# A hybrid decoder layer on one core: another order of the convolution, the compression's inputs and the compression in the input projection

## The chip, the core and the metric

The kernel runs on one core of a Trainium2 chip. The metric is device time in microseconds (us) from launch to the end of the program; several runs are made, and their median is told. The core's engines work side by side: TensorE (matrix products; PE in the profile, its weight loads PEld), VectorE (DVE), ScalarE (ACT), GpSimd (POOL) and SyncE (SP), which here only issues transfers. Each has its own queue of instructions and waits at semaphores for the others.

## The reference, cut to what matters

The layer takes a residual stream `x` of 512 positions and 2048 channels. It normalises it, multiplies it with one large input matrix `w_in`, and splits the columns of the product:

```python
proj = x @ w_in
q, k_c, v_c, k_s, v_s, k_w, v_w, g, u = jnp.split(proj, cuts, axis=-1)
gates = jax.nn.sigmoid(g)
kc = compress(kv_heads(k_c), cmp_pe_k, cmp_w1_k, cmp_w2_k)
vc = compress(kv_heads(v_c), cmp_pe_v, cmp_w1_v, cmp_w2_v)
o_nsa = nsa_attention(q, kc, vc, k_s, v_s, k_w, v_w, gates, rel_table)
o_conv = conformer_conv(u, conv_dw_w, conv_dw_b, conv_ln_g, conv_ln_b)
mix = jnp.concatenate([o_nsa, o_conv], axis=-1) @ w_out
```

`compress` takes windows of 32 positions of `k_c` (or `v_c`), multiplies them with a 2048x256 matrix, applies Gelu and multiplies with a 256x64 matrix. `conformer_conv` takes the 2048 columns `u`, multiplies one half with the Sigmoid of the other, applies a causal depthwise convolution of 31 taps to each of the 1024 channels, normalises over the channels and applies SiLU. Behind the mixer follow a cross-attention into 256 memory tokens and a mixture of 32 experts. The change touches only the order of work inside the input projection.

## The kernel before, in words

**One group of the projection.** `proj` (L102) computes up to 512 columns for all 512 positions. It loops over the 2048 input channels in 8 pieces of 256 (for a width of 512). For each piece `wtile` (L86) loads the weights into a ring buffer `wr` (three buffers, queue of SyncE) and splits them into a high and a low half, `wh` by ScalarE and `wl` by VectorE (L78, two buffers each). Each product is made of three (L82 to L84: high by high, high by low, low by high). They accumulate in four PSUM banks `pd`, one for each 128 columns, and a piece takes 24 products of 128x512. So a group takes 192. At the end `evac` empties the four banks. `hooks` names a function that is called before a given piece's weights; with it other work is laid between the pieces.

**The lead stage.** `mixer` (L330) loads `x`, normalises it, and `norm_T` (L166) turns it into 16 transposed chunks `xT`: four transposes (L172) into one of two PSUM banks of the tag "s", then ScalarE (L175) and VectorE (L176) read the bank, and VectorE subtracts (L177). The first group of the projection runs while these chunks come up. Then the pool `lnin` of the raw input closes, and other pools open: `cnv` for the convolution, `work`, and `cmp` for the compression.

**The compression's inputs.** `cmp_inputs` (L474) first clears `kcc` and `vcc` on GpSimd (L476, L477), loads and transposes the position vectors, and then runs the group for `k_c` and `v_c` (L503). It is the first group before the change. Its `evac` writes `kt` with 16 copies on ScalarE and 16 subtractions on VectorE (L501, L502).

**The convolution.** `conv_taps` (L409) loads the depthwise weights into a `wr` buffer (L414) and bias and norm vectors on GpSimd's queue (L417), transposes them on TensorE (L420, L423) into "s" banks, and copies them out to `wc` and `cvT` (L421, L424). Then it runs four groups of 512 columns: 256 of the first half and the matching 256 of the second. The eviction of a group makes two blocks of 128 channels. For each it takes the Sigmoid on ScalarE (L435), one of three `u` buffers, cleared at its head by GpSimd (L437), the product on VectorE (L438), which empties the two banks, and then 31 taps on VectorE (L441 and 30 times L443).

**The work between.** The generator `todo` chains `gate` (L508, two parts of 16 products), `compress` (L550, eight steps for keys and values, four each, of 24 products with 160 columns) and `mem_stats` (L275, four steps of statistics of the memory). The hooks of the convolution's groups take one step each: pieces 1 to 7 of group 0 and all pieces of the later groups. What is left is done behind group 3.

**Behind it** come `bias_setup`, `values` (L536, one group), `queries` for four heads (L595, groups of 384 columns, three banks, 144 products), and `conv_norm` (L447). The latter sums the channels with products against ones (L453, one pair of products for each block, `cmu`), subtracts the mean on VectorE (L459), squares, sums again (L462, `cvr`), and scales. From the second queries on, hooks bring in the transposed memory (`mem_T`, L289).

**What sets the order.** The program text gives each instruction a priority, and the builder fixes each engine's order from it, from readiness and from free buffers. `high_priority` with a positive offset moves instructions ahead, as for the weight splits and the first part of `conv_norm`; the taps have an offset of -100000, so they take what VectorE has left over:

```python
with tc.high_priority(offset=-100000):
    nc.vector.tensor_scalar(a, u[:, 0:S], wc[:, j, 0:1], vT[:, j:j + 1], op0=ALU.mult, op1=ALU.add)
    for k in range(1, CK):
        nc.vector.scalar_tensor_tensor(a, u[:, k:k + S], wc[:, j, k:k + 1], a, op0=ALU.mult, op1=ALU.add)
```

Of the kernel before, what the change touches and what calls it, by code (L numbers as in the profile page):

```python
# [22 lines left out]
S = 512  # L23
# [5 lines left out]
CW, CK = 1024, 31  # L29
# [23 lines left out]
class Kernel:  # L53
# [276 lines left out]
    def mixer(self):  # L330
        tc, nc, I = self.tc, self.nc, self.i
        w = I["w_in"][0]
        xh = lambda k, c: self.xT[k][:, 0, :] if c is None else self.xT[k][:, 0, c * P:(c + 1) * P]
        xl = lambda k, c: self.xT[k][:, 1, :] if c is None else self.xT[k][:, 1, c * P:(c + 1) * P]
        with ExitStack() as ctx:
            with ExitStack() as p1:
                self.psum(p1, d=4, s=2, t=1, o=1)
                xpb = p1.enter_context(self.pool("xpb", 6, True))
                xpa = p1.enter_context(self.pool("xpa", 10, True))
                with self.pool("lnin") as ln:  # L340
                    xs = [ln.tile([P, D], F32, name=f"xin{i}") for i in range(4)]
                    for i in range(4):
                        nc.sync.dma_start(xs[i], I["x"][0, i * P:(i + 1) * P, :])
                    gb = self.columns(ln, [I["ln_in_g"], I["ln_in_b"]], "xgb")
                    self.xT = [self.pg(xpa if k < 10 else xpb, f"xT{k}") for k in range(KC)]
                    for i in range(4):
                        self.normalise(xs[i], self.ln_stats(xs[i], self.inrs[:, i]))
                    self.norm_T(lambda i, k: xs[i][:, k * P:(k + 1) * P], 4, gb[:, 0], gb[:, 1], lambda k: (self.xT[k][:, 0, :], self.xT[k][:, 1, :]), ln, 6)
                cctx = p1.enter_context(ExitStack())
                cnv = cctx.enter_context(self.pool("cnv", 2, True))  # L350
                self.mctx = ExitStack()
                self.work = self.mctx.enter_context(self.pool("work"))
                self.kcc = self.work.tile([P, 2, NKV, 32], F32R, name="kcc")
                self.vcc = self.work.tile([32, NKV, P], F32R, name="vcc")
                self.gates = self.work.tile([P, 4, 48], F32, name="gates")
                with self.pool("cmp") as cp:
                    kt = self.cmp_inputs(cp, xh, xl, w)

                    todo = chain(self.gate(cp, xh, xl, w), self.compress(cp, kt), self.mem_stats())
                    kt = None  # L360
                    acc = self.conv_taps(cnv, xh, xl, w, lambda: next(todo, None))
                    for _ in todo:
                        pass
                self.bias_setup()
                self.mgb = self.columns(self.work, [I["mem_ln_g"][0], I["mem_ln_b"][0]], "mgb")
                vp = self.mctx.enter_context(self.pool("vp"))
                self.values(vp, xh, xl, w)
                self.kq = [self.queries(0, w, xh, xl)]
                self.conv_norm(acc, cnv)
                acc = None  # L370
                cctx.close()
                self.mpool = self.mctx.enter_context(self.pool("memT"))
                self.memT = []
                mt = p1.enter_context(self.pool("mtmp"))
                mem = lambda k: (lambda: self.mem_T(k, self.mpool, mt))
                for kv, hooks in ((1, HOOKS[0]), (2, HOOKS[1]), (3, {})):
                    self.kq.append(self.queries(kv, w, xh, xl, {n: mem(k) for n, k in hooks.items()}))
                self.xT = None

            with ExitStack() as p2:  # L380
                self.psum(p2, d=3, t=2, s=2, o=1)
                mp2 = self.mctx.enter_context(self.pool("memT2", 1, True))
                self.bmp = p2.enter_context(self.pool("bm", 3, True))
                self.kvp = p2.enter_context(self.pool("kvp", 2, True))
                self.mem_T(12, mp2, self.kvp, "t")
                self.att = p2.enter_context(self.pool("att", 2, True))
                self.mixT, self.heads = [None] * KC, []
                for kv in range(NKV):
                    pairs = self.attention(kv)
                    self.kq[kv] = None  # L390
                    if kv % 2 == 0:
                        m = self.bigt(0, f"mix{kv}")
                    for j in range(2):
                        k = 2 * kv + j
                        t = self.mixT[k] = m[:, k % 4]
                        self.split(t[:, 0, :], t[:, 1, :], pairs[j])
                self.wprio = 0
                for g in range(12):

                    h = PACE[g]  # L400
                    with tc.issue_after(self.heads[h].ins) if h >= 0 else ExitStack():
                        self.kv_group(g, "dve")
                self.wprio = 100000
        if "mix" in self.dbg:
            for k in range(KC):
                self.dump("mix", self.mixT[k].bitcast(F32), lambda a: a[k])


    def conv_taps(self, cnv, xh, xl, w, step):  # L409
        tc, nc, I = self.tc, self.nc, self.i  # L410
        wc = cnv.tile([P, 8, CK], F32, name="wc", bufs=1)
        vT = self.cvT = cnv.tile([P, 24], F32, name="cvT", bufs=1)
        nat = self.ring.tile([P, 1024], F32, tag="wr", bufs=self.RB, name="wr")[:CK]
        nc.gpsimd.dma_start(nat, I["conv_dw_w"][0].rearrange("k o c -> k (o c)"))  # L414
        vn = cnv.tile([24, P], F32, tag="sg", bufs=2, name="cvn")
        for j, nm in enumerate(("conv_dw_b", "conv_ln_g", "conv_ln_b")):
            nc.gpsimd.dma_start(vn[8 * j:8 * j + 8, :], I[nm][0].rearrange("(c p) -> c p", p=P))  # L417
        pt = self.ps()
        for c in range(8):
            nc.tensor.transpose(pt[:, c * 32:c * 32 + CK], nat[:, c * P:(c + 1) * P], self.ident[:CK, :CK])  # L420
        nc.vector.tensor_copy(wc, pt[:, :256].rearrange("p (c k) -> p c k", k=32)[:, :, :CK])  # L421
        pt = self.ps()
        nc.tensor.transpose(pt[:, :24], vn, self.ident[:24, :24])  # L423
        nc.vector.tensor_copy(vT, pt[:, :24])  # L424
        acc = [cnv.tile([P, 2, S], F32, name=f"acc{j}", bufs=1) for j in range(4)]
        for g in range(4):
            banks = {}

            def evac(c, bank):
                banks[c] = bank  # L430
                if c < 2:
                    return
                j = 2 * g + c - 2
                sg = cnv.tile([P, S], F32, tag="sg", bufs=2, name="sg")
                nc.scalar.activation(sg, bank, AF.Sigmoid)  # L435
                u = cnv.tile([P, CK - 1 + S], F32, tag="u", bufs=3, name="u")
                nc.gpsimd.memset(u[:, :CK - 1], 0.0)  # L437
                nc.vector.tensor_tensor(u[:, CK - 1:], banks[c - 2], sg, op=ALU.mult)  # L438
                a = acc[j // 2][:, j % 2, :]
                with tc.high_priority(offset=-100000):  # L440
                    nc.vector.tensor_scalar(a, u[:, 0:S], wc[:, j, 0:1], vT[:, j:j + 1], op0=ALU.mult, op1=ALU.add)  # L441
                    for k in range(1, CK):
                        nc.vector.scalar_tensor_tensor(a, u[:, k:k + S], wc[:, j, k:k + 1], a, op0=ALU.mult, op1=ALU.add)  # L443
            self.proj([(w, 2608 + 256 * g, 256), (w, 2608 + CW + 256 * g, 256)], 512, xh, xl, evac, False, 4, S, lo="dve", hooks={n: step for n in range(1 - min(g, 1), 8)})
        return acc

    def conv_norm(self, acc, work):  # L447
# [940 lines left out]
```

## Time and profile before

| what | value |
|---|---|
| median of 3 runs | 2642.68 us (2636.26 to 2644.41) |
| the profiled execution | 2640.3 us |
| its span, first to last instruction | 2638.5 us |
| TensorE busy | 2400.6 us |
| VectorE busy | 1136.0 us |
| ScalarE busy | 732.1 us |
| GpSimd busy | 192.9 us |
| mean granted TensorE clock | 0.964 |

Times in the rows count from the start of the span. "Busy" of an engine is the time in which it executed at least one instruction. A row of the timeline gives start, duration, engine, line, operation, tiles (written <- read), shapes and count; in square brackets stands how long the engine idled before it and what released it. A table by windows gives the same by stretches of time, with the granted clock of TensorE (1.00 is 2.4 GHz, 0.50 is 1.2 GHz) and the share of the 16 DMA engines.

### The profile page before, as it was taken

Reading aid. Unit: us, or ns where it says so; the run is one execution under the profiler, and the core shown is the slowest. Engines: PE = TensorE matmul, PEld = TensorE weight load, DVE = VectorE, ACT = ScalarE, POOL = GpSimd, SP = SyncE. Lnnn points to the kernel's source line nnn. Section 1 sums busy time; section 2 is a strip of 40 time slices with the busy share of each in tenths; the row PEclk is TensorE's granted clock in tenths of the full one; section 3 lists DMA queues with packets and bytes.
Section 4 is the critical chain, followed back from the end, with each engine's and each line's share of the span. In section 5 each row is a group of like instructions: output and inputs, shape, how many; then the busy total and the mean of one; then the engine's idle time right before and its main releaser. Section 6 shows DMA issues by size and latency. Waiting matters only on the chain. (4 is left out here: it accounts for less than half of the span.)

```text
span 2638.5 us, 31466 instructions
## 1 busy us (share of the span) xinstructions
PE 2400.6 (91%) x11314; PEld 1561.4 (59%) x11315; DVE 1136.0 (43%) x2406; ACT 732.1 (28%) x1294; POOL 192.9 (7%) x247
## 2 busy tenths in 40 slices
PE   6998898989999999999999968999998899999982
PEld 5786676779878778788888843333332334333320
DVE  5479985487877654543462442111110101101004
ACT  4332125376766522332321310101000001011003
POOL 1100000000000000000000120101000100111001
PEclk9999999999999999999999969999999999999996
DMA  3345233433234532333442397999999999999994
GB/s 138 102 141 160 72 79 108 122 108 121 92 117 129 198 128 96 135 106 101 180 155 97 120 372 314 417 416 411 407 409 406 412 398 415 340 403 414 415 411 165
DMA packets 194679, 615.22 MB, mean 233 GB/s; under 512 B 43147, under 2 KB 92483, under 8 KB 140978
## 3 DMA queue, kind: packets, MB, share of 16 engines
q1 hardware_dynamic: 176900, 563.90, 56.2%
q0 software_dynamic: 17296, 46.66, 5.8%
q8 instruction: 117, 1.92, 0.3%
q10 hardware_dynamic: 288, 2.10, 0.2%
q14 instruction: 78, 0.64, 0.1%
HBM read 591.56 MB, written 47.23 MB: 242 GB/s over the span
## 5 line engine op out<-in xcount | busy, mean ns | idle before, releaser
L1271 PE MATMUL gu<-mr,xeT 128*64 128x512 f32 x2048 | 542.2, 615 | 51.5 <-DMA mr<-moe_w_up 20.5
L78 DVE TENSOR_TENSOR wl<-wr,wh 128x1024 fp32r<-128x1024 f32 (+1 forms) x248 | 294.2, 1188 | 388.3 <-ACT wh L78 384.0
L78 ACT ACTIVATE wh<-wr 128x1024 fp32r<-128x1024 f32 (+1 forms) x250 | 256.0, 1026 | 633.3 <-PE pd L83 291.8
L1271 PEld LDWEIGHTS gu<-mr,xeT 128*64 128x64 f32 x2048 | 170.9, 140 | 358.3 <-issue 285.8
L1299 PE MATMUL dn<-mr,hT 128*64 128x512 f32 x1152 | 293.8, 601 | 14.5 <-PEq L1179 13.4
L1280 DVE TENSOR_TENSOR h<-gu,sg 64x256 f32<-64x256 f32 x72 | 30.7, 427 | 455.4 <-ACT sg L1279 454.8
L82 PE MATMUL pd<-xT,wh 128*128 128x512 f32 x512 | 201.9, 401 | 5.5 <-DVE v L546 2.2
L83 PE MATMUL pd<-xT,wh 128*128 128x512 f32 x512 | 204.0, 399 | 0.0
L1299 PEld LDWEIGHTS dn<-mr,hT 128*64 128x64 f32 x1152 | 91.0, 137 | 169.8 <-issue 151.5
L84 PE MATMUL pd<-xT,wl 128*128 128x512 f32 x512 | 183.6, 397 | 4.4 <-DVE wl L78 4.4
L1279 ACT ACTIVATE sg<-gu 64x256 f32<-64x256 f32 x72 | 27.0, 375 | 546.3 <-PE gu L1271 529.9
L443 DVE SCALAR_TENSOR_TENSOR acc<-u,wc,acc 128x512 f32<-128x512 f32 x240 | 164.2, 744 | 0.1
L1305 DVE TENSOR_SCALAR y<-dn,wlm 128x512 f32<-128x512 f32 x36 | 27.0, 751 | 228.4 <-PE dn L1299 212.2
L82 PEld LDWEIGHTS pd<-xT,wh 128*128 128x128 f32 x512 | 97.9, 191 | 31.6 <-issue 7.4
L84 PEld LDWEIGHTS pd<-xT,wl 128*128 128x128 f32 x512 | 97.1, 190 | 26.4 <-DVE wl L78 5.1
L1201 POOL DMA_INDIRECT acc_d<-y,ixm x36 | 56.9, 1580 | 731.3 <-DVE xeT L72 314.9
L83 PEld LDWEIGHTS pd<-xT,wh 128*128 128x128 f32 x512 | 97.4, 190 | 21.7 <-issue 2.4
L83 PE MATMUL pd<-x1T,wh 128*128 128x512 f32 x256 | 102.1, 400 | 0.0
L83 PE MATMUL pd<-wl,oT 128*128 128x512 f32 x256 | 100.0, 391 | 1.1 <-DVE wl L78 1.1
L84 PE MATMUL pd<-x1T,wl 128*128 128x512 f32 x256 | 100.9, 399 | 0.0
L82 PE MATMUL pd<-x1T,wh 128*128 128x512 f32 x256 | 99.2, 401 | 0.8 <-ACT x1T L175 0.8
L84 PE MATMUL pd<-wh,oT 128*128 128x512 f32 x256 | 99.8, 390 | 0.0
(414 smaller groups left out, 3954.4 us busy)
## 6 DMA issues: line engine op xcount, KB each, us to landing
mr<-moe_w_down SPq DMA_DIRECT2D x128, 1024.0 KB
mr<-moe_w_gate SPq DMA_DIRECT2D x127, 1024.0 KB
mr<-moe_w_up SPq DMA_DIRECT2D x127, 1024.0 KB
wr<-xa_wkv SPq DMA_DIRECT2D x64, 512.0 KB
wr<-w_in SPq DMA_DIRECT2D x112, 256.0 KB
wr<-w_out SPq DMA_DIRECT2D x32, 512.0 KB
wr<-xa_wq SPq DMA_DIRECT2D x32, 512.0 KB
wr<-xa_wo SPq DMA_DIRECT2D x32, 512.0 KB
```

The source lines that it names most:

```text
L78: return self.nc.scalar.activation(h, src, AF.Copy), eng.tensor_tensor(l, src, h.bitcast(F32), op=ALU.subtract)
L82: mm(out, lhsT=ah, rhs=bh, start=start, stop=False)
L83: mm(out, lhsT=ah, rhs=bl, start=False, stop=False)
L84: mm(out, lhsT=al, rhs=bh, start=False, stop=stop)
L443: nc.vector.scalar_tensor_tensor(a, u[:, k:k + S], wc[:, j, k:k + 1], a, op0=ALU.mult, op1=ALU.add)
L1201: self.nc.gpsimd.indirect_dma_start(out=self.acc_d.rearrange("s (h d) -> (s h) d", h=2), out_offset=bass.IndirectOffsetOnAxis(ap=ix, axis= ...
L1271: self.nc.tensor.matmul(bank[64 * a:64 * a + 64], lhsT=xT[:, 4 * q + c, :], rhs=w[a][:, c * 512:(c + 1) * 512], start=(q == c == 0), stop= ...
L1279: nc.scalar.activation(sg[64:128, sl], bank[0:64, sl], AF.Silu)
L1280: nc.vector.tensor_tensor(h[64 * b:64 * b + 64], bank[64:128, sl], sg[64:128, sl], op=ALU.mult)
L1299: self.nc.tensor.matmul(out[j][64 * a:64 * a + 64], lhsT=hT[:, r, :], rhs=w[:, 1024 * a + 512 * j:1024 * a + 512 * j + 512], start=(r == 0 ...
L1305: self.nc.vector.tensor_scalar(y[:, 512:], out[1], wl, None, op0=ALU.mult)
```

## The change

The convolution's weights are loaded and its group 0 runs first, in the lead stage, without hooks. Then `between` runs the compression's inputs and builds the chain of gate, compression and memory statistics. Groups 1 to 3 follow, each with a hook before each of its eight pieces. Nothing is added to or taken from the computation.

```diff
@@ mixer
                 with self.pool("cmp") as cp:
-                    kt = self.cmp_inputs(cp, xh, xl, w)
-
-                    todo = chain(self.gate(cp, xh, xl, w), self.compress(cp, kt), self.mem_stats())
-                    kt = None
-                    acc = self.conv_taps(cnv, xh, xl, w, lambda: next(todo, None))
-                    for _ in todo:
+
+                    todo = []
+
+                    def between():
+                        kt = self.cmp_inputs(cp, xh, xl, w)
+                        todo.append(chain(self.gate(cp, xh, xl, w), self.compress(cp, kt), self.mem_stats()))
+                    acc = self.conv_taps(cnv, xh, xl, w, lambda: next(todo[0], None), between)
+                    for _ in todo.pop():
                         pass
@@ conv_taps
-    def conv_taps(self, cnv, xh, xl, w, step):
+    def conv_taps(self, cnv, xh, xl, w, step, between):
...
-            self.proj([(w, 2608 + 256 * g, 256), (w, 2608 + CW + 256 * g, 256)], 512, xh, xl, evac, False, 4, S, lo="dve", hooks={n: step for n in range(1 - min(g, 1), 8)})
+            self.proj([(w, 2608 + 256 * g, 256), (w, 2608 + CW + 256 * g, 256)], 512, xh, xl, evac, False, 4, S, lo="dve", hooks={n: step for n in range(8 if g else 0)})
+            if g == 0:
+                between()
         return acc
```

## Rows read from the trace of the kernel before

**Rows 1.** The page: span, and busy time, share and instructions of each engine.
```profile
span 2638.5 us, 31466 instructions
PE 2400.6 (91%) x11314; PEld 1561.4 (59%) x11315; DVE 1136.0 (43%) x2406; ACT 732.1 (28%) x1294; POOL 192.9 (7%) x247
```

**Rows 2.** Busy time by windows, all engines; the first line names the columns.
```profile
core 0: us, PE busy (x) PEld busy (x) DVE busy (x) ACT busy (x) POOL busy (x), PEclk, DMA share, GB/s
23.60:76.50 52.90, 52.85 (x248) 43.86 (x248) 30.83 (x40) 19.85 (x25) 6.73 (x16) 1.00 0.21 65
76.50:150.30 73.80, 70.46 (x362) 59.15 (x362) 30.00 (x42) 29.72 (x45) 1.79 (x3) 0.98 0.37 108
...
206.50:231.40 24.90, 16.98 (x61) 12.21 (x61) 24.90 (x38) 3.58 (x4) 0.25 (x2) 0.79 0.78 219
231.40:262.30 30.90, 30.90 (x138) 25.42 (x137) 30.90 (x44) 5.95 (x7) 0.00 (x0) 1.00 0.40 117
262.30:307.80 45.50, 45.50 (x198) 36.81 (x198) 44.53 (x63) 9.67 (x11) 0.25 (x2) 1.00 0.32 94
307.80:334.20 26.40, 14.56 (x51) 10.37 (x51) 26.40 (x41) 2.49 (x3) 0.12 (x1) 0.74 0.07 20
```

**Rows 3.** Busy time by windows, VectorE alone (us, DVE busy, PEclk, DMA share, GB/s).
```profile
150.30:378.70 228.40, 221.31 (x360) 0.95 0.40 114
```

**Rows 4.** Timeline of TensorE, first stall: two pairs of the channel mean's products.
```profile
222.79 2.08 PE L453 MATMUL cmu<-acc,one 128*128 128x512 f32 x2 [7.92 <-DVE acc L443]
...
228.75 1.02 PE L453 MATMUL cmu<-acc,one 128*128 128x512 f32 x2
```

**Rows 5.** Timeline of GpSimd: the head of a `u` buffer is cleared.
```profile
222.79 0.13 POOL L437 MEMSET u<- 128x30 f32 x1 [31.62 <-DVE acc L443]
```

**Rows 6.** Timeline of TensorE, second stall.
```profile
328.01 2.08 PE L453 MATMUL cmu<-acc,one 128*128 128x512 f32 x2 [11.84 <-DVE acc L443]
```

**Rows 7.** Instructions of tile `pd` by windows (PE, PEld, DVE, ACT, PEclk, DMA share, GB/s).
```profile
206.50:231.40 24.90, 14.76 (x57) 11.33 (x57) 1.38 (x2) 0.58 (x1) 0.79 0.78 219
...
307.80:334.20 26.40, 12.64 (x49) 9.69 (x48) 1.35 (x2) 0.58 (x1) 0.74 0.07 20
...
411.00:430.00 19.00, 9.70 (x32) 6.76 (x31) 5.36 (x8) 4.70 (x8) 0.73 0.43 151
```

**Rows 8.** Groups of VectorE, 76.5 to 380 us: busy, mean ns | idle before.
```profile
L443 DVE SCALAR_TENSOR_TENSOR acc<-u,wc,acc 128x512 f32<-128x512 f32 x240 | 164.2, 744 | 0.1
L78 DVE TENSOR_TENSOR wl<-wr,wh 128x1024 fp32r<-128x1024 f32 x47 | 57.4, 1221 | 41.4 <-ACT wh L78 41.3
...
L438 DVE TENSOR_TENSOR u<-pd,sg 128x512 f32<-128x512 f32 x8 | 5.5, 686 | 3.0 <-ACT sg L435 3.0
...
L441 DVE TENSOR_SCALAR acc<-u,wc,cvT 128x512 f32<-128x512 f32 x8 | 4.3, 542 | 0.1
```

**Rows 9.** Timeline of TensorE between the compression's inputs and the gate.
```profile
79.62 0.68 PE L420 MATMUL ptr<-ident,wr 31*128 31x31 f32 x8 [2.77 <-ACT pe L68]
...
80.92 0.74 PE L520 MATMUL pdg<-xT,wh 128*96 128x512 f32 x1 [0.57 <-DVE wh L78]
```

**Rows 10.** Timelines of TensorE and VectorE: the channel mean's last pair, the mean's subtractions.
```profile
379.47 1.02 PE L453 MATMUL cmu<-acc,one 128*128 128x512 f32 x2
...
381.24 4.90 DVE L459 TENSOR_TENSOR acc<-acc,mus 128x512 f32<-128x512 f32 x8
```

**Rows 11.** Groups of the lead stage, 23.6 to 72 us.
```profile
L176 DVE TENSOR_SCALAR nv<-ptr,xgb 128x512 f32<-128x512 f32 x16 | 12.3, 806 | 3.6 <-ACT xT L175 3.2
...
L175 ACT ACTIVATE xT<-ptr,xgb 128x512 fp32r<-128x512 f32 x15 | 11.0, 774 | 5.0 <-PE ptr L172 4.9
...
L476 POOL MEMSET kcc<- 128x256 f32 x1 | 0.3, 305 | 14.8 <-DVE xT L177 14.8
```

## The prediction, made before the changed kernel was run

> **What bounds the kernel now.** I read the page first: the span is 2638.5 us and TensorE is busy for 91% of it [rows 1], so time can come back only where TensorE stands still or runs slowly. The profiled execution took 2640.3 us, 2.4 below the median of the three runs, 2642.7; the sum is made against 2640.3 and moved up by 2.4 at the end. The change touches nothing behind the mixer, so I cut the mixer's first half into windows [rows 2]. The reader is to see there two windows in which TensorE is not full while VectorE is: 206.5 to 231.4 (17.0 of 24.9 us busy, VectorE 24.9) and 307.8 to 334.2 (14.6 of 26.4, VectorE 26.4). Against them stands 76.5 to 150.3, where VectorE works for 30.0 of 73.8 us. From 150.3 to the last tap at 378.7 VectorE is busy for 221.3 of 228.4 us [rows 3], 97%: that stretch is bound by the taps, and the stretch before it has room for some of them.
>
> The chain of one stall is in the timeline. At 222.79 TensorE starts a product of the channel mean after 7.92 us of idling for a tap [rows 4]; at the same moment GpSimd, after 31.62 us, gets a `u` buffer that a tap releases [rows 5]. There are three `u` buffers, and a conv group needs two: the second eviction of a group waits until the first block of the group before is through its 31 taps, and a PSUM bank stays occupied until then. The second stall is the same at 328.01, 11.84 us of idling [rows 6].
>
> **What the change removes.** First the size of the stalls. A product of 128x512 costs 30.9 us / 138 = 0.224 us in the undisturbed window 231.4 to 262.3 [rows 2]; a pair of the channel mean's costs at most 1.0 [rows 4]. Stall 1: 57 products [rows 7] x 0.224 = 12.8, two pairs 2.0, so 24.9 - 14.8 = 10.1 us. Stall 2: 49 x 0.224 = 11.0, one pair 1.0, so 26.4 - 12.0 = 14.4. Together 24.5. The idling alone is 7.9 + 11.8 = 19.8; the other 4.7 are products at the lower clock, since the granted clock is 0.79 and 0.74 of 2.4 GHz in these windows and 1.00 in the one between them [rows 2]. The Trainium skill (TensorE: Matmul & The Clock Gate, Part 1, What's actually happening) says that the throttled clock is the default and activity releases it; by it a stall costs more than its idling, 24.5 rather than the 19.8 that counting idle time would give, and the windows agree.
>
> **Whether the stalls go.** A block of 128 channels costs VectorE (164.2 + 5.5 + 4.3) / 8 = 21.8 us [rows 8]; eight are 174. After the change the first two blocks (43.5) are released at about 76.5, not 150. Then come the compression's inputs, 192 products, 43.0 us, and group 1 with eight hooks: that is the present 76.5 to 150.3 (group 0 with two gate parts and five compression steps) plus one more step. Of the 73.8 us, 43.0 are products of the group, 7.2 the gate's 32, 4.4 the hand-over up to 80.92 [rows 9], so a step with its small products is (73.8 - 54.6) / 5 = 3.8. Group 1 then ends at 76.5 + 43.0 + 77.6 = 197. VectorE has until then the present 30.0, nine more splits of 1.2 [rows 8] and 43.5 of taps: 84 of 121 us. It fits, with 36 us idle. Group 2 (43.0 + two steps) ends near 248 and group 3 near 293. The stall at the end of group 1 needs block 0, long done; that at the end of group 2 needs block 2, done by 235. That at the end of group 3 needs block 4: 65 us of taps and some 29 of splits and statistics, 94 of the 96 us from 197 to 293. That is a tie, but a late bank is covered: in stall 1 TensorE went on from 206.5 to 214.9 on its other banks. I take both stalls as gone, -24.5; the lower bound of the gain is stall 1 alone, 10.1.
>
> **What it adds and moves.** The new hand-over from group 0 to the compression's inputs: its nearest row is group 2 to group 3, inside 262.3 to 307.8, where TensorE is busy for all 45.5 us [rows 2]. I take 0; the upper bound is the 4.4 of rows 9, which itself stays and only moves behind the inputs. The 16 subtractions of the inputs' eviction now meet left-over taps on VectorE, but the taps have the lower priority; 0, at most one tap each. Table loads on ScalarE: the two Gelu's still lie between Sigmoids, no change. DMA: group 0's weights come as two transfers per tile instead of one, the inputs' the other way round; over a lead stage whose DMA share is 0.21 [rows 2] I take 0. On GpSimd's queue the depthwise weights' load moves ahead of the stage and the clearing of `kcc` behind the convolution's vectors; GpSimd is idle for most of this. On SyncE the same loads stand in another order, each still held by a ring buffer.
>
> **What is late next** is the convolution's norm. VectorE has 251.3 us of work from 76.5 to the last tap (30.0 + 221.3); 84 are done by 197, the other 167 at 97% end near 369. Now it is 378.7. So the taps end only some 10 us sooner while TensorE is 24 ahead, and the norm, which now meets the first queries' products, meets the border between the first and second queries. There 4.9 us of subtractions [rows 10] go before the queries' eviction. One of four banks is spare; 12 products in it cover 2.7. I take 2.2 for the rest, between 0 and the 11.8 that 411 to 430 loses now (19.0 less 32 x 0.224) [rows 2, 7].
>
> **Sum:** 2640.3 - 24.5 + 2.2 = 2618.0; as a median 2620. About 0.3%, 8 us, is what a measurement of this kernel can tell from no change.
>
> **The rivals.** (a) The end of the taps sets the end: TensorE's queue has the channel mean's last pair and the variance products between the queries' products, and whatever stands behind a waiting one waits too. Now the last pair starts at 379.47 without an idle gap [rows 10]. If it is placed ahead of TensorE's independent work, the gain shrinks to the 0 to 10 us by which the taps end sooner: 2633 to 2643, most likely 2638. For it: VectorE's work is not lessened, and both present stalls are such waits. Against it: three more groups of queries lie there to fill with. The Trainium skill (Perfetto Trace Analysis, Identifying the Most-Contended Engine) calls the engine of highest occupancy the one to optimise first; that would be VectorE here, whose work the change leaves alone, and by that rule the result is this one. The 43.8 us that VectorE idles before 150.3 [rows 2] speak against the rule.
>
> (b) Only stall 1 goes whole, because block 4 is late by more than its cover: 10 to 17 us gained, 2626 to 2633.
>
> (c) Slower: the lead stage loses its second transposing bank. The depthwise weights' load and transposes now stand ahead of group 0; TensorE is idle early, so they can be issued before the normalised input's transposes, into one of the same two PSUM banks. The copy out goes to `wc`, in a pool opened after the input's pool is closed; such tiles wait now: the clearing of `kcc` waits 14.8 us for the last input transpose's subtraction [rows 11]. With one bank for 16 chunks each turn is the four transposes (about 0.5) and both readers at 0.77 and 0.81 us [rows 11], which read one after the other at worst: 2.1 x 16 = 33 us if nothing covers it. It turns the result slower than before beyond 22 us exposed; whole, it gives 2640.3 - 22.3 + 33 + 2.4 = 2653. Against it: a chunk has 12 products, 2.7 us, to run meanwhile, and TensorE is busy for 52.85 of 52.9 us of that stage [rows 2].
>
> (d) The change does not do what it says: if the builder's order puts the taps behind the compression all the same, nothing moves, 2643.
>
> **How the numbers follow.** Forecast 0.54 (2609 to 2627: from all of the 24.5, with a kinder border than the 411 to 430 of now, to a border that costs 9); (b) 0.14; (a) 0.16; (d) 0.03; (c) 0.13. Faster by over 0.3% means below 2634.8: forecast, (b) and a quarter of (a), 0.72. Within: the rest of (a), (d), and cases of (c) with about 22 exposed, 0.15. Slower, above 2650.6: 0.13, all from (c). The range runs from 2609 to 2642, leaving out most of (c) and edges of (a) and (d).
>
> **What would show it.** Right: taps begin near 77; VectorE is busy about 84 of 121 us up to the end of group 1; no TensorE gap over 3 us at the three borders between groups or into the values; granted clock near 1.00 from 80 to 340; the last tap near 369. Wrong: a wait of TensorE on a tap of over 5 us anywhere (a, b); gaps in front of the input's transposes before 76 and a lead stage of over 60 us (c); the first tap still near 150 (d).

## The result and the profile after

The changed kernel takes 2628.06 us (median of 4 runs, 2624.23 to 2629.35) against 2643.14 for the kernel before in the same series (4 runs, 2636.26 to 2644.41): a ratio of 0.9946, 95% interval [0.9926, 0.9966]. It is faster by 15 us where 22 were forecast. The time lies inside the range, but eight us behind the forecast, in the stretch that rival (b), "only one stall goes whole", had given.

The page of the profiled execution (2624.23 us, the fastest of the four) answers [rows 1]; the engines do the same work as before.

```profile
span 2622.6 us, 31465 instructions
PE 2395.1 (91%) x11314; PEld 1564.2 (60%) x11315; DVE 1135.9 (43%) x2406; ACT 733.3 (28%) x1294; POOL 191.3 (7%) x247
```

The next view is the busy time by windows, cut at the new borders; it answers [rows 2]. The columns are the window, its length, busy time of PE, PEld, DVE, ACT and POOL, the granted clock, the DMA share and GB/s.

```profile
23.60:76.50 52.90, 52.74 (x252) 43.76 (x253) 30.74 (x40) 18.35 (x23) 5.90 (x15) 1.00 0.26 81
79.50:122.00 42.50, 42.50 (x188) 34.63 (x187) 41.38 (x61) 9.94 (x17) 1.50 (x2) 1.00 0.30 87
122.00:204.30 82.30, 76.67 (x391) 64.44 (x390) 41.43 (x55) 30.96 (x42) 0.56 (x3) 0.98 0.35 103
204.30:258.00 53.70, 53.70 (x270) 44.32 (x269) 50.93 (x109) 15.95 (x20) 2.75 (x4) 1.00 0.58 169
258.00:282.00 24.00, 16.09 (x55) 11.36 (x54) 24.00 (x37) 2.46 (x3) 0.25 (x2) 0.79 0.63 173
282.00:314.00 32.00, 32.00 (x142) 26.36 (x141) 30.94 (x43) 6.67 (x7) 0.00 (x0) 1.00 0.38 114
314.00:334.20 20.20, 20.00 (x86) 15.62 (x85) 20.20 (x30) 3.97 (x5) 0.12 (x1) 1.00 0.26 79
344.00:364.00 20.00, 15.43 (x68) 12.41 (x67) 19.71 (x35) 5.46 (x16) 0.00 (x0) 1.00 0.28 67
```

From 204 to 258 TensorE is busy all the time, and behind group 3 (314.0 to 334.2) for 20.00 of 20.20 us. But 258 to 282 has the face of the old stalls: TensorE 16.09 of 24.00 us, VectorE all of it, a granted clock of 0.79. The timelines of TensorE and GpSimd name it. L457 is the old L453, L439 the old L437, L445 the old L443.

```profile
273.15 2.07 PE L457 MATMUL cmu<-acc,one 128*128 128x512 f32 x2 [7.91 <-DVE acc L445]
```

```profile
142.47 0.12 POOL L439 MEMSET u<- 128x30 f32 x1 [57.11 <-DVE acc L445]
144.69 0.12 POOL L439 MEMSET u<- 128x30 f32 x1 [2.11 <-DVE acc L445]
...
273.16 0.13 POOL L439 MEMSET u<- 128x30 f32 x1 [39.19 <-DVE acc L445]
277.53 0.12 POOL L439 MEMSET u<- 128x30 f32 x1 [4.24 <-DVE acc L445]
317.67 0.12 POOL L439 MEMSET u<- 128x30 f32 x1 [40.02 <-DVE acc L445]
```

This is [rows 4] and [rows 5] again, 50 us later: the same 7.9 us, the same 273.15 on both engines. The stall of the end of group 1 has moved to the end of group 2; the one of [rows 6] is gone. The five clearings also tell why. Blocks 0 and 1 give their buffers back 2.2 us apart, blocks 2 and 3 4.4 us apart: VectorE filters the two blocks of a group in turns, tap by tap, so the first of a pair is through only when the second nearly is.

Read as a chain, in milestones (the start of the second Sigmoid of a group for its end, of the first eviction for values and queries; us from the start of each profiled span):

| stage ends | before | after | length before | length after |
|---|---|---|---|---|
| group 1 | 207.4 | 204.3 | | |
| group 2 | 263.2 | 257.8 | 55.8 | 53.5 |
| group 3 | 308.6 | 314.2 | 45.4 | 56.4 |
| values | 364.9 | 356.1 | 56.3 | 41.9 |
| first queries | 411.2 | 403.3 | 46.3 | 47.2 |
| second queries | 456.9 | 445.2 | 45.7 | 41.9 |
| fourth queries (with the third) | 528.6 | 519.9 | 71.7 | 74.7 |

The values come 14.4 us sooner after group 3, just the size worked out for stall 2, and group 3 comes 11.0 later after group 2, about the size worked out for stall 1. At the last queries 8.7 us of the gain stand.

### The profile page after: what moved, and what is told of

Same layout as the page of the kernel before. It is cut to its first block, busy times and chain, and to the rows that moved or that the text cites. A ratio compares the mean times of both kernels' runs of the same rounds, so it can differ in the third digit from the quotient of the medians.

```text
span 2622.6 us, 31465 instructions
## 1 busy us (share of the span) xinstructions
PE 2395.1 (91%) x11314; PEld 1564.2 (60%) x11315; DVE 1135.9 (43%) x2406; ACT 733.3 (28%) x1294; POOL 191.3 (7%) x247
## 5 line engine op out<-in xcount | busy, mean ns | idle before, releaser
L1275 PE MATMUL gu<-mr,xeT 128*64 128x512 f32 x2048 | 535.0, 607 | 53.5 <-DMA mr<-moe_w_up 24.3
L78 ACT ACTIVATE wh<-wr 128x1024 fp32r<-128x1024 f32 (+2 forms) x250 | 256.0, 1026 | 619.6 <-PE pd L83 287.2
L1303 PE MATMUL dn<-mr,hT 128*64 128x512 f32 x1152 | 294.7, 602 | 14.8 <-PEq L1183 12.1
L445 DVE SCALAR_TENSOR_TENSOR acc<-u,wc,acc 128x512 f32<-128x512 f32 x240 | 164.7, 745 | 0.3
```

The costliest lines, as they stand in the source:

```text
L78: return self.nc.scalar.activation(h, src, AF.Copy), eng.tensor_tensor(l, src, h.bitcast(F32), op=ALU.subtract)
L1275: self.nc.tensor.matmul(bank[64 * a:64 * a + 64], lhsT=xT[:, 4 * q + c, :], rhs=w[a][:, c * 512:(c + 1) * 512], start=(q == c == 0), stop= ...
L1303: self.nc.tensor.matmul(out[j][64 * a:64 * a + 64], lhsT=hT[:, r, :], rhs=w[:, 1024 * a + 512 * j:1024 * a + 512 * j + 512], start=(r == 0 ...
```

## The experiments

All ratios are against the kernel before, with their 95% intervals.

| run | median us (runs) | ratio |
|---|---|---|
| changed, six `u` buffers | 2610.56 (5) | 0.9877 [0.9860, 0.9894] |
| before, six `u` buffers | 2634.03 (9) | 0.9964 [0.9951, 0.9976] |
| changed, blocks one after the other | 2632.24 (6) | 0.9956 [0.9942, 0.9970] |
| before, only the hooks moved | 2623.90 (6) | 0.9923 [0.9909, 0.9937] |
| changed once more | 2627.87 (6) | 0.9939 [0.9917, 0.9962] |
| changed, inputs behind group 1 | 2629.50 (6) | 0.9940 [0.9920, 0.9959] |
| the same, six `u` buffers | 2616.48 (6) | 0.9899 [0.9878, 0.9920] |
| the same, one buffer more (block 3) | 2623.40 (6) | 0.9922 [0.9900, 0.9944] |
| hooks moved, six `u` buffers | 2609.05 (5) | 0.9863 [0.9841, 0.9885] |
| changed, two buffers more (blocks 1, 5; "five `u`") | 2610.08 (5) | 0.9867 [0.9845, 0.9889] |
| that, bias table built early | 2626.56 (6) | 0.9933 [0.9909, 0.9956] |
| that, its stores spread out | 2615.56 (6) | 0.9903 [0.9887, 0.9919] |

### Is it the `u` buffer? Six of them

```diff
+                    self.cp = cp
-                u = cnv.tile([P, CK - 1 + S], F32, tag="u", bufs=3, name="u")
+                u = self.cp.tile([P, CK - 1 + S], F32, name=f"u{j}") if j in (1, 3, 5) else cnv.tile([P, CK - 1 + S], F32, tag="u", bufs=3, name="u")
```

> The changed kernel, with u buffers of their own for blocks 1, 3 and 5 (six in all instead of three). Theory: the stall that is left, 7.9 us of idling at 265 to 273 plus products at the lower clock, some 10 us in all, is the wait of block 5's u for the buffer of block 2, whose 31 taps end only with those of block 3 because the two run in turns. With six buffers the four banks are free at the end of group 2: no TensorE gap over 2 us from 140 to 350, 8 to 11 us less than the changed kernel, about 2618 where that has 2628. Rival 1: it is the channel mean's pair standing in TensorE's queue that waits for the tap, whatever the buffers; then the 7.9 us stay and the time is 2628 within 3. Rival 2: VectorE bounds the stretch; the gap goes, but TensorE loses the same 8 to 10 us later, before 420, and the time is 2628 within 3.

2610.56 us. The windows at the place of the stall are full, and group 3 ends at 303.1 in place of 314.2:

```profile
258.00:282.00 24.00, 24.00 (x105) 19.52 (x104) 24.00 (x35) 4.56 (x5) 0.12 (x1) 1.00 0.30 87
282.00:303.00 21.00, 21.00 (x92) 16.87 (x91) 20.34 (x29) 4.61 (x5) 0.00 (x0) 1.00 0.34 101
```

So the moved stall was a wait for a buffer, nothing else, and removing it beats both kernels. But the whole gains 17.5 us where 8 to 11 were expected, and only 8.9 of them stand at the fourth queries (511.0 against 519.9). Some 10 more come in the stage behind, the attention's heads, which the edit does not name. This is that stage by windows, from the fourth queries to the load of the next norm's vectors, in the changed kernel and with six buffers:

```profile
519.87:894.56 374.69, 357.68 (x2229) 311.93 (x2228) 285.56 (x855) 254.92 (x576) 21.78 (x38) 0.96 0.37 115
511.01:875.55 364.54, 350.87 (x2229) 305.79 (x2228) 283.00 (x855) 254.79 (x576) 21.52 (x38) 0.98 0.38 118
```

The instructions are the same in number, but the traces have VectorE's in another order. TensorE waits 13.3 us in sum where it waited 16.8, at a granted clock of 0.98 where it had 0.96. Why the builder chose that order, and what each exchange is worth, was not tested. A new wait of 10.9 us comes up at the values' eviction; it is taken up below.

The same edit on the kernel before:

> The kernel before with six u buffers (blocks 1, 3 and 5 have their own). Theory: both of its stalls (10.1 and 14.4 us) are waits for a u buffer and go as gaps between groups, but here VectorE is busy without a break from 150 on, so part of it comes back: the last tap stays within 5 us of 378.7, TensorE reaches the norm some 20 us earlier, and the time falls by 10 to 22, to 2621 to 2633. Rival: where VectorE is busy without a break, buffers give nothing, since TensorE only runs into the end of the taps: 2643 within 4.

2634.03 us. The two stalls at the groups' ends shrink here too (group 3 ends at 298.0), but the gain is given back at once: the fourth queries come at 529.6, in the kernel before at 528.6. The windows view and the waits of TensorE (us in total, times, longest):

```profile
300.00:370.00 70.00, 48.12 (x194) 36.58 (x193) 70.00 (x144) 11.70 (x24) 1.18 (x2) 0.84 0.33 85
```

```profile
PE pd L82 <- DVE v L547: 13.3, 1, 13.3
PE cmu L454 <- DVE acc L444: 7.1, 2, 5.2
```

VectorE is busy for all 70 us, with taps that began only at 152.3. But the wait of 13.3 us has another cause beside it, as the timelines of GpSimd and ScalarE show:

```profile
352.67 0.56 POOL L258 DMA_DIRECT2D tab<-rel_table  x1 [65.53 <-DVE acc L444]
```

```profile
360.95 0.79 ACT L68 ACTIVATE v<-pd 128x128 fp32r<-128x128 f32 x4 [17.29 <-DMA vec_d<-vec]
```

The extra buffers lie in the compression's pool and hold it until a tap gives it back at 352; only then is the table of position biases loaded (at 184 in the kernel before), and the values' first eviction waits for its store. So this run does not settle what more buffers are worth in the old order: the place that they were given costs time itself. As they stand here they are worth 10 us of the median (0.4%), in the changed order 17.

### Do the taps' turns hold the buffer? One block after the other

```diff
+        self.lastap = None
-                with tc.high_priority(offset=-100000):
+                with tc.high_priority(offset=-100000), (tc.issue_after(self.lastap.ins) if self.lastap else ExitStack()):
-                        nc.vector.scalar_tensor_tensor(...)
+                        self.lastap = nc.vector.scalar_tensor_tensor(...)
```

> The changed kernel, with the taps of each block put behind the last tap of the block before, so that a pair is not run in turns. Theory: block 2 is then through its taps near 240 instead of 273, its u buffer is free before group 2 ends at 257, and the stall goes as with more buffers: 2617 to 2621 where the changed kernel has 2628. GpSimd's clearing for block 5 then stands near 240 and that for block 7 before 310. Rival: the pair in turns is not what holds the buffer (VectorE is simply short of time before 257): block 2 still ends after 260, the stall stays, 2628 within 3. A worse case is that a tap that follows its own predecessor at once takes longer than 0.667 us; at 10% more VectorE loses 16 us in all and the time is above 2628.

2632.24 us. Block 2 now gives its buffer back at 244, and the stall at the end of group 2 goes (group 3 ends 44.8 us behind group 2, where the changed kernel has 56.4):

```profile
244.03 0.13 POOL L440 MEMSET u<- 128x30 f32 x1 [14.97 <-DVE acc L446]
```

That is the direct proof for the turns. But the last tap ends at 415.6, 37 us later, and the whole gains nothing. One reason is in the timeline of VectorE: six taps of one block in a row, and six in turns of two blocks in the changed kernel:

```profile
245.95 4.68 DVE L446 SCALAR_TENSOR_TENSOR acc<-u,wc,acc 128x512 f32<-128x512 f32 x6
```

```profile
248.16 4.06 DVE L445 SCALAR_TENSOR_TENSOR acc<-u,wc,acc 128x512 f32<-128x512 f32 x6
```

A tap that follows its own predecessor comes every 0.78 us; with another block's tap between them, every 0.67. The groups of VectorE behind 204 us, here and in the changed kernel, give the sum for 180 taps:

```profile
L446 DVE SCALAR_TENSOR_TENSOR acc<-u,wc,acc 128x512 f32<-128x512 f32 x180 | 134.7, 749 | 4.3
L445 DVE SCALAR_TENSOR_TENSOR acc<-u,wc,acc 128x512 f32<-128x512 f32 x180 | 123.4, 745 | 0.0
```

So slower taps are 11.3 of the 37 us. By the busy time of the two stretches 14 more are other work that here comes before the last tap, splits of the queries' weights above all, and 12 are idling of VectorE. The turns save 8% of the taps' time there and cost a buffer's early return.

### Which part of the change acts? The hooks alone

```diff
-            self.proj(..., hooks={n: step for n in range(1 - min(g, 1), 8)})
+            self.proj(..., hooks={n: step for n in range(8 if g else 0)})
```

This is the kernel before, inputs first, with the first convolution group freed of hooks.

> The kernel before, with one part of the change alone: the compression's inputs lead as before, group 0 follows without hooks, and gate, compression and statistics lie between the pieces of groups 1 to 3. The first taps then start near 125 instead of 150 (changed kernel: 79). Theory: in the changed kernel VectorE has 36 us to spare in group 1, so the 46 us between 79 and 125 buy little; blocks 0 and 1 are still done by 180, before group 1 ends, and the rest runs as in the changed kernel: 2628 within 4, with a gap at the end of group 2 of about 8 us. Rival: the early start is what counts; without it the taps end some 40 us later or the stall at the end of group 1 stays, and the time is near 2643.

2623.90 us, no worse than the full change. The first tap starts at 130.8, not at 79.5, and yet group 1 ends at 203.7, the same stall comes at the same place, and the last tap ends at 378.1:

```profile
191.61 0.12 POOL L437 MEMSET u<- 128x30 f32 x1 [8.14 <-DVE acc L443]
193.85 0.12 POOL L437 MEMSET u<- 128x30 f32 x1 [2.11 <-DVE acc L443]
...
272.56 0.13 POOL L437 MEMSET u<- 128x30 f32 x1 [39.19 <-DVE acc L443]
```

What acts, as I read it, is that group 0 ends 21 us earlier without hooks while group 1 ends where it did: with the compression's products between its weights group 1 lasts about 72 us while pair 0/1 is filtered; in the kernel before it lasted 55 (from 152.2 to 207.4). Whether that pair was started 50 us earlier still makes no difference. To see whether the 4 us between this run and the changed kernel are real, that one ran again:

> The changed kernel once more, unchanged, beside the others: 2624 to 2630. If it comes to 2624 here, the kernel with the hooks alone (2623.9) is level with it; if it stays at 2628, leading with the convolution's group costs some 4 us rather than nothing.

2627.87 us; the intervals of the two ratios overlap. The part "the convolution's first group leads" shows no gain. Nor do the traces show a cost of it in the projection: the second queries come at 445.2 in both kernels. The 4 us lie in the heads again, which take 371.1 us here and 374.7 and 373.5 in the two executions of the changed kernel. With the buffers out of the way (three more, as above):

> The inputs lead as in the kernel before, only the first group's hooks are taken out (gate and compression start in group 1), and blocks 1, 3 and 5 get u buffers of their own. If leading with the convolution's group is worth nothing in itself (as with three buffers, 2623.9 against 2628.1), this gives the 2610.6 of the changed kernel with six u buffers, 2607 to 2614. Rival: the earlier first taps (81 against 131 us) are what pays once the buffers are no longer short, since VectorE is then busy to the end of the taps; then the taps end some 5 to 10 us later here, the values' evictions wait for VectorE as in the kernel before with six u buffers (13 us), and the time is 2618 to 2626.

2609.05 us against 2610.56: the rival, by which the early taps would pay then, falls too.

### The inputs one group later

Groups 0 and 1, then the inputs, then groups 2 and 3 with the hooks, so that taps run from 80 without a break:

```diff
-            self.proj(..., hooks={n: step for n in range(8 if g else 0)})
-            if g == 0:
+            self.proj(..., hooks={n: step for n in range(8 if g > 1 else 0)})
+            if g == 1:
                 between()
```

> Order: convolution groups 0 and 1, then the compression's inputs, then groups 2 and 3 with gate and compression between their weights; still three u buffers. Theory (a pair of blocks is filtered in turns, so its u buffers come free only when the whole pair ends, about 41 us of taps after it began; a group that follows earlier than that on the next group but one stalls): pair 0/1 starts near 80 and ends near 122 to 125, when group 1 ends; pair 2/3 ends near 170 to 185, while the inputs stage and group 2 run; groups 2 and 3 end near 222 and 300. No group's end waits over 3 us for a u buffer, the 7.9 us wait of the changed kernel near 273 is gone, the last tap ends 15 to 40 us earlier than 378, and the time is 2606 to 2616. Rival 1 (the wait is only moved again): blocks 2 and 3 wait at the end of group 1, 6 us or more, and the time is that of the changed kernel, 2624 to 2632. Rival 2 (VectorE's total sets the last tap wherever the groups stand): the last tap stays within 5 us of 378 and the time is over 2618.

2629.50 us: rival 1 by its time, though no single wait is over 5 us. Pair 0/1 was not through by 125 but by 133 to 138, and the waits of TensorE from 115 to 345 (us in total, times, longest) are

```profile
PE cmu L457 <- DVE acc L445: 4.6, 1, 4.6
PE pd L82 <- DVE u L440: 4.5, 1, 4.5
PE pdg L523 <- ACT wh L78: 2.4, 1, 2.4
PE pd L82 <- DVE kt L506: 2.4, 1, 2.4
```

The first two are for buffers, at the ends of groups 3 and 1, and the other two stand at the hand-over behind the inputs.

> As the run before (groups 0 and 1, inputs, groups 2 and 3), and blocks 1, 3 and 5 get u buffers of their own. Theory: no buffer is short in that order, so this gives nothing more: within 4 us of the run before. Rival: a buffer was still waited for at the end of group 1; then this is faster by the length of that wait, 4 to 10 us.

2616.48 us, 13 less: the theory that no buffer is short in that order falls as well.

> Groups 0 and 1, then the inputs, then groups 2 and 3, with one u buffer more, for block 3 alone. That block is filtered long before group 2, so nothing holds the compression's pool late. Theory: the wait of 4.5 us at the end of group 1 that three buffers left in this order (2629.5) goes, the table of biases is no longer late as with six (2616.5, where its stores at 333 to 349 meet the weights' loads), and the time is 2606 to 2613. Rival: this order loses by something else (the hand-overs after the inputs, the table's stores beside the weights wherever they fall); then it stays at 2614 or above.

2623.40 us: rival. One buffer for block 3 removes one of the two 4.5 us waits (group 2 ends at 246.9 where three buffers gave 254.0), but its view of waits still has 4.6 for a tap at `cmu`, at the end of group 3. None of the three beats the simpler order with more buffers.

### The wait that comes up at the values

Only blocks 1 and 5 need a buffer of their own, if the reasoning on pairs is right:

> The changed kernel with u buffers of their own for blocks 1 and 5 only; the other six share three. Blocks 0, 2 and 3 hold the three; block 4 follows block 0 (free near 142), blocks 6 and 7 follow blocks 2 and 3, whose pair ends near 273, before group 3 ends near 303. Theory: no wait for a u buffer is left, so the time is that of the changed kernel with six, 2608 to 2613, or up to 3 us less as less of the pool that the biases are built in is held by late blocks. Rival: the sixth buffer matters: a wait of 3 us or more at the end of group 3 and a time of 2614 to 2620.

2610.08 us, as with six. The 10.9 us wait is there as before. The timelines of GpSimd, VectorE and ScalarE in the run with six buffers show what leads up to it:

```profile
340.38 0.56 POOL L258 DMA_DIRECT2D tab<-rel_table  x1 [65.73 <-DVE acc L446]
```

```profile
347.72 2.40 DVE L267 COPY vec<-tabT 16x1 f32<-16x1 f32 x32
```

```profile
352.01 0.79 ACT L68 ACTIVATE v<-pd 128x128 fp32r<-128x128 f32 x4 [1.67 <-DMA vec_d<-vec]
```

The table of position biases is loaded when the last tap of block 5 gives the compression's pool back, at 340; then it is transposed, copied and stored, and the first value tile waits for the end of that store. The next run builds the table between the groups, in the compression's pool, where it shares a buffer with the gates' tile:

```diff
-                        todo.append(chain(..., self.mem_stats()))
+                        todo.append(chain(..., self.mem_stats(), self.bias_setup(cp)))
-                self.bias_setup()
```

> The changed kernel with u buffers of their own for blocks 1 and 5 (2610.1), and the table of position biases built as the last step between the groups' weights, in the compression's pool, and not after that pool is given back. In the runs with five and six buffers block 5's buffer kept that pool until 340 us; the table's load, two transposes, 32 copies on VectorE and its store followed from there one behind the other, and the values' first eviction came at 352 behind them, a 10.9 us wait of TensorE. Theory: that chain is the wait, so here the table is done by 270 as in the changed kernel, the wait at the values' eviction falls to the 2 to 5 us that VectorE's subtractions cost, and the time is 2601 to 2606. Rival: VectorE, busy with the taps until about 380, sets the stretch anyway (the norm's sum over channels needs the last tap); then the 6 to 8 us come back as waits before the second query group and the time stays within 3 us of 2610.

2626.56 us, 16 slower; neither theory had that. The timelines of SyncE and ScalarE show a new wait at the end of group 2:

```profile
235.25 16.07 SPq L271 DMA_DIRECT2D toe_d<-vec_d  x16
252.09 45.80 SPq L92 DMA_DIRECT2D wr<-w_in  x20
```

```profile
262.12 1.06 ACT L78 ACTIVATE wh<-wr 128x1024 fp32r<-128x1024 f32 x1 [15.05 <-DMA wr<-w_in]
```

The sixteen stores of the table stand in one row on SyncE's queue, and ScalarE waits 15.05 us for the weights behind them; TensorE waits 8.1 us for a Sigmoid that ScalarE can't reach. In the run with five buffers the same row of stores (352 to 368) lay beside the 10.9 us wait, and the weights had run ahead by then, so I take it that one wait had hidden the other. The last run spreads the stores:

```diff
-        for h in range(NH):
-            nc.sync.dma_start(self.toe_d[...], ...)
-        yield
+        for h in range(0, NH, 2):
+            with tc.issue_after(self.wload.ins):
+                for g in (h, h + 1):
+                    nc.sync.dma_start(self.toe_d[...], ...)
+            yield
```

> As the run with the table of biases built between the groups' weights (2626.6), but its sixteen stores go two by two, each pair behind one of the weights' loads of the last two groups, where that run had all sixteen in one row on SP (16.1 us from 235 to 251) with the next weights' loads behind them: the first of those landed 15 us late for ScalarE, and TensorE lost 8.1 us at the end of group 2. Theory: the order on SP is the cost, not the bytes; spread out, the stores cost 2 us or less, group 2 ends near 258 and group 3 near 303 as with five buffers (2610.1), the values' first eviction no longer waits behind the table's chain (10.9 there, 2 to 6 here), and the time is 2601 to 2607. Rival 1: VectorE sets this stretch until the last tap near 380, so what the values gain comes back before the second query group, and the time is 2607 to 2613. Rival 2: the bytes are the cost (5.2 MB beside the weights); then the groups' ends stay late by 5 us or more and the time is 2615 or above.

2615.56 us. The theory holds for its cause. The windows of TensorE from 240 to 260 (busy time, clock, DMA share, GB/s), first with the stores in a row, then spread:

```profile
240.00:260.00 20.00, 17.07 (x76) 0.99 1.05 259
```

```profile
240.00:260.00 20.00, 20.00 (x90) 1.00 0.95 266
```

About the same GB/s, and TensorE is full. Group 2 ends at 258.8, group 3 at 304.2, the values' first eviction comes at 347.7 (352.3 with five buffers), the first queries' at 390.3 (398.0). TensorE's wait at the values is 6.8 us, a little over the 2 to 6 expected.

Then rival 1 takes it in its outcome: the second queries come at 437.0, against 437.2. (The time itself lies in rival 2's stretch, but the groups' ends are not late.) The last tap ends at 381.0, so the norm's SiLUs end within 3 us of the other runs, the one with the table early apart. On ScalarE the rounding of a weight piece stands behind seven of them, at 423.49, and its split on VectorE behind that. Only then, at 425.35, does SyncE issue the next weights into a freed buffer; they reach ScalarE at 431.47, and TensorE has waited 2.94 us:

```profile
418.53 5.06 ACT L477 ACTIVATE acc<-acc,cvT 128x512 f32<-128x512 f32 x7
423.49 0.83 ACT L78 ACTIVATE wh<-wr 128x768 fp32r<-128x768 f32 x1
...
431.47 0.84 ACT L78 ACTIVATE wh<-wr 128x768 fp32r<-128x768 f32 x1 [2.17 <-DMA wr<-w_in]
```

```profile
424.36 0.96 DVE L78 TENSOR_TENSOR wl<-wr,wh 128x768 fp32r<-128x768 f32 x1 [2.09 <-ACT wh L78]
```

```profile
425.35 9.38 SPq L92 DMA_DIRECT2D wr<-w_in  x6
```

```profile
432.37 0.79 PE L82 MATMUL pd<-xT,wh 128*128 128x512 f32 x1 [2.94 <-ACT wh L78]
```

The wait is not all: the stage from the first to the second queries lasts 46.8 us here and 39.2 with five buffers. Some 2 us of it are four more variance products, and from 430 to 437 the granted clock is 0.60 (1.00 with five buffers).

The medians of these two, 2610.08 and 2615.56, come from different series; their intervals touch, and the two profiled spans are 2613.2 and 2613.9, of which the first is the slowest of its five executions. The last run shows no gain, and a small loss is likelier than none.

One table for all of this (us, milestones as above; "SiLU" is the end of the convolution's last one):

| | before | after | hooks alone | five `u` | table early | stores spread |
|---|---|---|---|---|---|---|
| group 3 | 308.6 | 314.2 | 313.2 | 303.4 | 313.6 | 304.2 |
| values | 364.9 | 356.1 | 355.1 | 352.3 | 355.6 | 347.7 |
| first queries | 411.2 | 403.3 | 403.7 | 398.0 | 399.1 | 390.3 |
| last tap ends | 378.1 | 378.5 | 378.1 | 382.1 | 389.8 | 381.0 |
| SiLU | 427.5 | 427.1 | 427.8 | 426.8 | 433.8 | 425.0 |
| second queries | 456.9 | 445.2 | 445.2 | 437.2 | 446.0 | 437.0 |

## Why the prediction was right or wrong

**The stalls' cause and size: right.** Both were waits for a `u` buffer, as read from [rows 4] to [rows 6]; six buffers remove what is left. Stall 2 was priced at 14.4 us and gave 56.3 - 41.9 = 14.4. The two stages have the same products in them, so this agreement is not chance. That a stall costs more than its idling showed again at the lower granted clock (0.79 in the window of the moved one: 11.0 us for 7.9 of idling).

**The step that failed** is "that at the end of group 2 needs block 2, done by 235". It counted a block as 21.8 us of VectorE behind its start, as if blocks were filtered one after the other. They run in pairs, in turns; block 2 is through at 273.16, 38 us later than I said and 15 after its buffer is asked for. Run one after the other, the buffer came back at 244 and the stall was gone. The rows of before could have told: in [rows 5] the buffer of block 0 comes free only at 222.79, after 31.62 us of waiting, some 70 us behind the first tap. So stall 1 was not removed but moved, and the sum had 10.1 us too much. That is rival (b)'s outcome, one stall of two, with another stall than the one it named: block 4 was not late. By the prediction's own signs, too, the wait of 7.9 us on a tap stands for "wrong".

**Where luck helped.** The sum's 22.3 us were to stand at the queries; 8.7 do. The median's 15 has the rest from behind them, where the sum had nothing. That the time comes within 8 us of the forecast, and into (b)'s stretch, is in part luck.

**Group 1's end** was put at 197 and came at 204.3. Of the 7.3 us, 3 are group 0, which ended at 79.5 and not at 76.5; its hand-over to the inputs cost 0.7, near the 0 taken. The window 122.0 to 204.3 lost 82.3 - 76.7 = 5.6 us, mostly behind the inputs, where 4.4 was to stay, so 1.2 more. The two long waits there look as the last two rows that the run with the inputs one group later shows above, 2.4 us each; one is for a `kt` subtraction, and these now stand between taps on VectorE. The 0 for them was too small. The last 2.4 us lie in TensorE's busy time and were not taken apart.

**VectorE's room: right.** Up to 204.3 it is busy for 41.38 + 41.43 = 82.8 us (forecast 84). **The last tap** was to come at 369 and ends at 378.5, as before. From 204.3 on 170.05 us are left and run at 170.05 / 174.2 = 98%: the amount is what was worked out (167), but it starts 7 us later. Before that VectorE idles for 42 us, most of it because the taps of blocks 0 and 1 are done (142 to 145) and group 1 delivers the next only at 203.

**Late next.** The norm was to cost 2.2 us at the border of the first and second queries. That stage got 3.8 shorter and the queries after it 3.0 longer, -0.8 in all. The values' eviction, costed at nothing, waits 5.3 us for VectorE (2.2 before), since its subtractions alternate with taps.

**The rivals.** (a), the taps' end sets the end, falls for this change: the last tap did not move and the second queries came 11.7 us sooner. A later form of it is shown by the last run: near 437 the norm does hold the second queries. The Trainium skill (Perfetto Trace Analysis, Identifying the Most-Contended Engine) calls the engine with the highest occupancy the one to optimise first. In this stretch that is VectorE; its work and its last tap stayed, and 8.7 us were gained up to the fourth queries all the same, 16.2 with five buffers, so here the runs speak against the rule. (c) falls: TensorE is busy for 52.74 of 52.90 us in the lead stage, against 52.85 in [rows 2]. (d) falls, since the first tap is at 79.5; but of the two things that the change does, the runs show a gain for one only, the hooks' new place.

**What stays open.** 8.7 us stand at the fourth queries. At their ends the two profiled executions of the changed kernel are 15.9 and 12.1 us ahead of the one of before. In the first, 6.3 of that came in the experts, where this execution alone is fast (1120.3 us from their setup to the end; 1126.7 before, 1125.2 to 1126.8 in every other run). In the second only 1.5 came there. So the traces show some 10 us for the change up to the experts (9.6 and 10.7), and what the medians have beyond that is not traced to it: the executions of the kernel before run from 2634.8 to 2650.6, and one of them has a trace. Why the heads' order changes with edits in front of it, and gives 3 us in one run and 10 in another, is open too.

## What to carry to other kernels

A buffer is free when the consumer that the scheduler interleaves with its neighbours is through, not after its own work's length: read the release times of the pairs in the trace before dating one. When a stall is taken out, look at what lay beneath it (here a row of stores and a norm) and at whether the same buffer is asked for once more a stage later. Compare milestones and not only end times: here half of what the buffers gave came in a stage that the edit did not name. And split a change into its parts on the chip: here one line of hooks carried all of it.

## What the runs showed of the hardware

A dependent chain on VectorE was slower than two in turns: 4.68 us for six taps of 128x512 against 4.06, or a tap every 0.78 and every 0.67 us. Sixteen stores of 320 KB in a row held SyncE's queue for 16.07 us, and ScalarE waited 15.05 us for the weights queued behind them; in pairs between the loads, at a DMA share of 0.95 from 240 to 260 us, they cost TensorE nothing there. In this case it was the place in the queue, not the bytes.
